# Down projection of six token tiles from seven block products instead of eight, with loads held back in the order pass

## The chip, the cores and the metric

The kernel runs on one core of one Trainium2 chip. The metric is the device time of one execution in microseconds (us), the median over runs. A core has five engines that run side by side, each with its own instruction list that it works through in order: TensorE (PE: matmuls, and PEld, its weight loads), VectorE (DVE), ScalarE (ACT), GpSimd (POOL) and SyncE (SP). In this kernel SP issues every DMA. Data lie in device memory, in the on-chip buffer SBUF (128 partitions), and matmuls write to PSUM, which has 8 banks of 128 partitions x 512 floats.

## The reference, cut to what matters

One inference step of a two-part layer (a token mixer, then a gated feed-forward block with a causal convolution) on 1024 prompt tokens and 32 sample tokens, all in float32. The change lies in the last matrix product.

```
def conv_ffn(xn, buf, w_up, conv_w, conv_b, w_down):
    up = xn @ w_up                                  # 1024 -> 2 * 2816
    up, buf = causal_dwconv(up, buf, conv_w, conv_b)
    gate, val = jnp.split(up, 2, axis=-1)
    return (jax.nn.gelu(gate, approximate=True) * val) @ w_down, buf   # 2816 -> 1024
...
x = x + rms_norm(h, g_mix_post[l])
h, ffn_buf = conv_ffn(rms_norm(x, g_ffn_pre[l]), states[6][l], ffn_w_up[l], ffn_conv_w[l], ffn_conv_b[l], ffn_w_down[l])
x = x + rms_norm(h, g_ffn_post[l])
```

## The kernel before, in words

**Tiles.** The 1056 tokens are nine tiles `u`: 0 to 7 are 128 prompt tokens each, 8 is the 32 sample tokens. The 2816 hidden features are `NF` = 22 tiles `f` of 128. Every float32 matrix product is done as three matmuls of rounded halves (`mm3`, L87 to L89): an operand is split into a high half (a cast on ACT, L93) and the remainder (a subtraction on DVE, L96). So each operand of a product costs one ACT and one DVE instruction before PE can use it.

**Stages.** By time: input projection and token mixer with the output projection (0 to about 640 us), up projection (about 640 to 1104 us), down projection (from 1096 us to the end).

**Up projection** (`up_block`, `up_finish`). For each `f` the gate tile and the value tile are computed in a seven-product form over two column ranges (`SUBS`) into `uu`; it is kept in `puy`, `pux`, `puw`, `puz` of PSUM and added out by DVE (L1197). `up_finish` then copies halo columns (POOL, L1229 to L1232), does the three-tap convolution (ACT L1233, two DVE L1235 per half), the GELU (ACT L1237), the product (DVE L1238), and stores the result of 128 features x 1060 columns to device memory as `h_d[f]` (L1239). `up_operands` makes the operand sums for the next `f` (DVE L1163 to L1169) and their splits.

**Down projection** (`down_all`). Three token groups (`DGROUPS`) are worked through one after the other, each over all 22 `f`. For every `f`, `load_h` loads the group's columns of `h_d[f]` into `hr` and the 128 x 1024 weight tile into `wd_..r` (L1302, L1307), both with two buffers, and splits them: one split of `hr`, two of the weight tile.

- The first group (tiles 0, 1 and the 32 sample tokens, 288 columns) has the weights as the stationary operand: 8 banks `pd` of 128 output features x 288 columns, 24 matmuls per `f`. Its result is copied to `accd`, turned by PE transposes (`pt`, L1350) and finished.
- The second and third group (tiles 2 to 4, tiles 5 to 7) have the tokens as the stationary operand: 6 banks `pd` of 128 tokens x 512 output features, 18 matmuls per `f`, 22 times.

`finish` (L1289 to L1297) squares a tile's result on ACT, multiplies by the gain `gp` on DVE, forms the reciprocal root on POOL (L207, L208), scales and adds the residual `fr` on DVE, and stores it.

**What sets the order.** The program is first recorded in the order of the Python code. Then `order` builds a graph of the instructions and `play` walks it as a list scheduler with fixed costs: each engine takes, among the instructions that are ready, the one with the longest remaining path (`tails`; `AHEAD` adds to the priority of some pools). The resulting sequence is fixed for every engine, SP's list of DMAs among them. An engine never reorders at run time: when the next instruction waits, everything behind it on that engine waits too. In `play`, `queue` stands for the time at which all DMAs issued so far would be through.

Of the kernel before, what the change touches and what calls it, by code (L numbers as in the profile page):

```python
# [36 lines left out]
DGROUPS = [(0, 1, 8), (2, 3, 4), (5, 6, 7)]  # L37
# [40 lines left out]
def body(ctx: ExitStack, tc: tile.TileContext, a: dict):  # L78
# [47 lines left out]
    h_d = dr.tile([NF, 128, NCOL], F32, name="h_d")  # L126

# [1094 lines left out]

    def up_finish(py, f, uu):

        ys = []
        for i, j in enumerate((f, NF + f)):
            u = uu[i][:, 2:]
            y = py.tile([128, NCOL], F32, tag="y", name=f"y{j}", bufs=3)
# [10 lines left out]
        sp.dma_start(h_d[f], ys[0])  # L1239

# [31 lines left out]
    def down_all(ph, p6, gp):  # L1272
        xres = {}

        def residual(u):
            n = 128 if u < 8 else DEC
            x = p6.tile([128, 1024], F32, tag="xres", name=f"fr{u}", bufs=4)
            sp.dma_start(x[:n], x2_d[128 * u:128 * u + n, :])
            xres[u] = x

        def finish(u, n, src):

            x = xres.pop(u)
            ss = p6.tile([128, 4], F32, tag="fss", name=f"gss{u}", bufs=2)
            jk = p6.tile([128, 1024], BF16, tag="fjk", name=f"gjk{u}", bufs=2)
            ys = []
            for hf in range(2):
                c = slice(512 * hf, 512 * hf + 512)
                act.activation(jk[:n, c], src[hf], AF.Square, scale=1.0 / 32, accum_out=ss[:n, 2 + hf:3 + hf])  # L1289
                y = p6.tile([128, 512], F32, tag="yt", name=f"yt{u}{hf}", bufs=4)  # L1290
                dve.tensor_tensor(y[:n], src[hf], gp[:n, c], op=ALU.mult)
                ys.append(y)
# [6 lines left out]
        def load_h(g, f, spans, w):  # L1299
            r = ph.tile([128, 384], F32, tag="hr", name=f"hr{g}_{f}", bufs=2)  # L1300
            for (c0, c1, o) in spans:
                sp.dma_start(r[:, o:o + c1 - c0], h_d[f, :, c0:c1])  # L1302
            hh = ph.tile([128, 384], F32R, tag="hh", name=f"hh{g}_{f}", bufs=2)
            hl = ph.tile([128, 384], F32R, tag="hl", name=f"hl{g}_{f}", bufs=2)
            split(hh[:, :w], hl[:, :w], r[:, :w], dve)
            wr = praw[0].tile([128, 1024], F32, tag="raw", name=f"wd{g}_{f}r", bufs=2)
            sp.dma_start(wr, a["w_dn"][f])  # L1307
            return hh, hl, [weight_halves(f"wd{g}_{f}{hf}", wr[:, 512 * hf:512 * hf + 512]) for hf in range(2)]

        def spans_of(us):  # L1310
            spans, off, w = [], {}, 0
            for u in us:
                n = 128 if u < 8 else DEC
                off[u] = w
                if spans and spans[-1][1] == fcol(u):
                    spans[-1][1] += n
                else:
                    spans.append([fcol(u), fcol(u) + n, w])
                w += n
            return spans, off, w  # L1320

        def banks_of(g, m):

            where = [(psf, "xw", 4)] * 4 + [(psb, "big", 3)] * 3 + [(psf, "sx", 1)]
            return [p.tile([128, 512], F32, tag=t, name=f"pd{g}_{i}", bufs=b) for i, (p, t, b) in enumerate(where[:m])]


        us = DGROUPS[0]
        spans, off, w = spans_of(us)
        banks = banks_of(0, 8)  # L1330
        for f in range(NF):
            hh, hl, wd = load_h(0, f, spans, w)
            if f == NF - 4:
                for u in us:
# [4 lines left out]
        acc = p6.tile([128, 8, 288], F32, name="accd")  # L1339
        for d in range(8):  # L1340
            (act.copy if d % 2 else dve.tensor_copy)(acc[:, d, :], banks[d][:, :w])

        def turned(u):
            n = 128 if u < 8 else DEC
            src = []
            for hf in range(2):
                p, t, b = ((psb, "big", 3), (psf, "sx", 1))[hf]
                ps = p.tile([128, 512], F32, tag=t, name=f"pt{u}{hf}", bufs=b)
                for d in range(4):
                    pe.transpose(ps[:n, 128 * d:128 * d + 128], acc[:, 4 * hf + d, off[u]:off[u] + n], ident)  # L1350
# [670 lines left out]
```

## Time and profile before

| | |
|---|---|
| median of 3 runs | 1376.55 us (1372.03, 1376.55, 1376.82) |
| the profiled execution | 1371.32 us |
| its span, first to last instruction | 1369.5 us |
| mean granted TensorE clock | 0.997 of full |
| PE busy, share of span | 1324.6 us, 97% |
| DVE busy, share of span | 986.7 us, 72% |
| ACT busy, share of span | 702.2 us, 51% |
| DMA | 255.13 MB, mean 186 GB/s |

The profile is of one execution, which took 1371.32 us; its span is 1.8 us shorter. A row of the groups reads: line, engine, operation, output tile <- input tiles, shapes, count | busy us, mean ns of one | idle time of the engine before them and what ended it. Successive instructions of one engine overlap, so the mean ns of one is longer than the distance from start to start. A row of the stretches gives for each piece of the span the busy time of PE, PEld, DVE, ACT and POOL with the number of instructions in brackets, then the granted clock, the busy share of the DMA engines and the rate in GB/s.

### The profile page before, as it was taken

How to read it: one execution, taken by the hardware profiler on the slowest of the kernel's cores; microseconds unless marked ns; L12 is line 12 of the kernel's file. 1: busy time of each engine (PE TensorE's matmuls, PEld its weight loads, DVE VectorE, ACT ScalarE, POOL GpSimd, SP SyncE). 2: the span in 40 equal slices, each digit the busy share in tenths (PEclk: the TensorE clock that was granted, in tenths of full speed). 3: DMA queues.
4: the chain of work that ended last, by engine and by line, in shares of the span. 5: the costliest groups of instructions: out<-in, count | busy, mean ns of one | idle time of the engine just before them, and what ended most of it. 6: DMA issues, size and time to landing. Idle time of an engine off the chain costs nothing.

```text
span 1369.5 us, 30222 instructions
## 1 busy us (share of the span) xinstructions
PE 1324.6 (97%) x12076; PEld 1223.9 (89%) x12076; DVE 986.7 (72%) x1765; ACT 702.2 (51%) x1369; POOL 171.8 (13%) x331
## 2 busy tenths in 40 slices
PE   6999999999999899999899999999999999999998
PEld 5999999998899777778899999999999999888786
DVE  6785549757888477877988887887887765545644
ACT  5554566445575454436654454454454455444443
POOL 2010001100102012222011111111111100000200
PEclk9999999999999999999999999999999999999999
DMA  8899789986898863634122221222221377656853
GB/s 319 270 330 323 249 279 316 295 262 196 312 298 274 299 225 116 211 107 157 48 91 82 80 79 71 86 78 71 87 78 67 106 239 228 193 170 190 291 176 102
DMA packets 130851, 255.13 MB, mean 186 GB/s; under 512 B 28087, under 2 KB 76887, under 8 KB 130711
## 3 DMA queue, kind: packets, MB, share of 16 engines
q1 hardware_dynamic: 130711, 253.21, 55.5%
q8 instruction: 94, 1.54, 0.5%
q14 instruction: 46, 0.38, 0.1%
HBM read 192.01 MB, written 61.16 MB: 185 GB/s over the span
## 4 chain that ended last, share of the span: by engine, by line
PE 80%; DVE 8%; DMA 7%; ACT 2%; issue 1%; SPq 0%; POOL 0%; DVEq 0%; ACTq 0%; POOLq 0%
PE pd L87 6%; PE pd L88 6%; PE pd L89 6%; PE pux L89 4%; PE pux L87 4%; PE pux L88 4%; PE pv L87 4%; PE pv L89 4%; PE pv L88 4%; PE puw L88 3%; PE puw L89 3%; PE puw L87 3%; PE pf L87 3%; PE pf L89 3%; PE pf L88 3%; PE zp L87 2%
## 5 line engine op out<-in xcount | busy, mean ns | idle before, releaser
L1235 DVE SCALAR_TENSOR_TENSOR y<-uu,fconv_sb,y 128x1060 f32<-128x1060 f32 x88 | 116.1, 1321 | 11.2 <-ACT y L1233 10.5
L87 PE MATMUL pd<-wd,hh 128*128 128x512 f32 x264 | 77.8, 396 | 0.7 <-ACT hh L93 0.7
L88 PE MATMUL pd<-wd,hh 128*128 128x512 f32 x264 | 77.8, 396 | 0.0
L89 PE MATMUL pd<-wd,hl 128*128 128x512 f32 x264 | 77.0, 396 | 0.0
L1233 ACT ACTIVATE y<-uu,fconv_sb 128x1060 f32<-128x1060 f32 x44 | 56.0, 1275 | 20.1 <-POOL uu L1230 20.1
L922 POOL TENSOR_TENSOR hrs<-hss,mhalf 128x5 f32<-128x5 f32 (+3 forms) x27 | 40.5, 1505 | 180.9 <-DVE hss L921 180.9
L96 DVE TENSOR_TENSOR hl<-hr,hh 128x384 fp32r<-128x384 f32 (+1 forms) x66 | 34.5, 523 | 39.1 <-PE pd L89 23.7
L87 PEld LDWEIGHTS pd<-wd,hh 128*128 128x128 f32 x264 | 49.4, 188 | 13.2 <-ACT hh L93 1.1
L89 PEld LDWEIGHTS pd<-wd,hl 128*128 128x128 f32 x264 | 49.3, 188 | 12.0
L88 PEld LDWEIGHTS pd<-wd,hh 128*128 128x128 f32 x264 | 49.4, 188 | 11.7
L1192 ACT COPY c<-pux 128x274 f32<-128x274 f32 (+1 forms) x132 | 46.0, 381 | 25.1 <-PE pux L89 24.3
L87 PE MATMUL pv<-wt_0h,xh 128*128 128x256 f32 (+2 forms) x195 | 53.3, 298 | 3.4 <-DVE xl L305 1.7
L93 ACT CAST hh<-hr 128x384 fp32r<-128x384 f32 (+1 forms) x66 | 32.0, 486 | 43.1 <-PE pd L88 30.2
L89 PE MATMUL pv<-wt_0h,xl 128*128 128x256 f32 (+2 forms) x195 | 51.3, 289 | 0.0
L88 PE MATMUL pv<-wt_0l,xh 128*128 128x256 f32 (+2 forms) x195 | 51.2, 287 | 0.0
L87 PE MATMUL pv<-wt_1h,xh 128*128 128x256 f32 (+2 forms) x195 | 49.1, 288 | 0.4 <-ACT xh L304 0.4
L89 PE MATMUL pv<-wt_1h,xl 128*128 128x256 f32 (+2 forms) x195 | 48.6, 289 | 0.8 <-DVE xl L305 0.8
L88 PE MATMUL pv<-wt_1l,xh 128*128 128x256 f32 (+2 forms) x195 | 48.1, 287 | 0.0
L1230 POOL COPY uu<-fcache_sb 128x2 f32<-128x2 f32 x44 | 16.1, 366 | 192.0 <-DVE uu L1197 192.0
L87 PEld LDWEIGHTS pv<-wt_0h,xh 128*128 128x128 f32 (+1 forms) x195 | 34.9, 189 | 5.4 <-DVE xl L305 1.8
L207 POOL TENSOR_SCALAR gss<-gss 128x1 f32<-128x1 f32 (+1 forms) x9 | 6.7, 745 | 243.8 <-ACT gjk L1289 243.8
L89 PEld LDWEIGHTS pv<-wt_0h,xl 128*128 128x128 f32 (+1 forms) x195 | 34.9, 189 | 0.7 <-DVE xl L305 0.2
(1720 smaller groups left out, 4971.4 us busy)
## 6 DMA issues: line engine op xcount, KB each, us to landing
h_d<-y SPq DMA_DIRECT2D x22, 530.0 KB, 2.8
wt_0r<-in_w_tok SPq DMA_DIRECT2D x21, 512.0 KB, 6.1
wt_1r<-in_w_tok SPq DMA_DIRECT2D x21, 512.0 KB, 5.7
wt_0l<-lt_d SPq DMA_DIRECT2D x14, 512.0 KB, 7.5
wt_1l<-lt_d SPq DMA_DIRECT2D x14, 512.0 KB, 5.9
qkb<-qkb_d SPq DMA_DIRECT2D x8, 768.0 KB, 7.5
hr<-h_d SPq DMA_DIRECT2D x44, 128.0 KB, 3.1
hr<-h_d SPq DMA_DIRECT2D x22, 192.0 KB, 3.4
```

Of the source, the lines that this page charges most:

```text
L87: pe.matmul(ps, lh[0], rh[0], start=first, stop=False, **kw)
L88: pe.matmul(ps, lh[0], rh[1], start=False, stop=False, **kw)
L89: return pe.matmul(ps, lh[1], rh[0], start=False, stop=last, **kw)
L93: act.copy(hi, src)
L96: (eng or pool).tensor_tensor(lo, src, hi.bitcast(F32), op=ALU.subtract)
L207: pool.tensor_scalar(out, ss, other, EPS, op0=ALU.add, op1=ALU.add)
L922: pool.tensor_tensor(rs[:n, h0:h0 + nh], ss[:n, h0:h0 + nh], mhalf[:n, :nh], op=ALU.pow)
L1192: act.copy(t, ps)
L1230: pool.tensor_copy(u[:, GAP_S:GAP_S + 2], fcache[:, j, :])
L1233: act.activation(y, u, AF.Identity, scale=fconv[:, j, 2:3], bias=fconv[:, j, 3:4])
L1235: dve.scalar_tensor_tensor(y, uu[i][:, s:s + NCOL], fconv[:, j, s:s + 1], y, op0=ALU.mult, op1=ALU.add)
```

## The change

Tokens are regrouped: the first group is now tiles 0, 8 and 4 (`FIRST`), still done in the direct form. Tiles 1 to 3 (`UPPER`) and 5 to 7 (`LOWER`) are done together as a 2 x 2 block product: rows are upper and lower tokens, the inner dimension is taken in `NP` = 11 pairs of `f` (even and odd), and the columns are the two halves of the 1024 outputs. The eight block products of the direct form are replaced by seven products of sums of blocks (`seven`, called for p1, p2, p6, p5, p3, p7, p4), each over 11 pairs and three token tiles.

- **Sums of the left operand** are made in `up_finish` after every odd `f`: four DVE instructions on 128 x 384, stored as `s_d`.
- **Sums of the weights** are made by `sums`: four DVE instructions on 128 x 512 and two stores of 512 KB to `t_d` per pair. Six pairs are done during the up projection from two extra loads each (`EARLY`), five during the first group from the weight tiles that are loaded there anyway.
- **Loads of the passes**: 128 x 384 of the left operand and 128 x 512 of the right into one tile `r` with three buffers; one split of each.
- **Results** are combined from PSUM by ACT copies and DVE additions into `cu` and `cl`, and finished in halves (`finish_half`, `finish_end`).
- **Buffers**: the weight tiles of the first group rotate over 4 new `wide` buffers (the first two over the old pair), pools change sides, `gp` and the residuals of the first group are requested two `f` earlier, the product tile `y` of the value half has one buffer of its own.
- **The order pass**: names get priorities of their own (`AHEAD`), and SP takes no further DMA while the modelled DMA backlog is more than `BACKLOG` = 2000 ns. This holds for the whole program, so lists of the earlier stages change as well.

```diff
-DGROUPS = [(0, 1, 8), (2, 3, 4), (5, 6, 7)]
+FIRST, UPPER, LOWER = (0, 8, 4), (1, 2, 3), (5, 6, 7)
+NP = NF // 2
+EARLY = (0, 2, 4, 5, 7, 9)
...
+    def sums(k, ws):
+        (b11, b12), (b21, b22) = ((t[:, :512], t[:, 512:]) for t in ws)
+        dve.tensor_tensor(b11, b12, b11, op=ALU.subtract)
+        dve.tensor_tensor(b12, b22, b12, op=ALU.subtract)
+        dve.tensor_tensor(b22, b22, b11, op=ALU.subtract)
+        dve.tensor_tensor(b21, b21, b22, op=ALU.subtract)
+        for i in range(2):
+            sp.dma_start(t_d[k, i], ws[i])
...
         sp.dma_start(h_d[f], ys[0])
+        if f % 2 == 0:
+            even[0] = ys[0]
+            return
+        (a11, a21), (a12, a22) = ([t[:, fcol(us[0]):fcol(us[0]) + 384] for us in (UPPER, LOWER)] for t in (even[0], ys[0]))
+        st = py.tile([128, 3, 384], F32, tag="st", name=f"st{f}", bufs=1)
+        s1, s2, s3, s4 = st[:, 0], a11, st[:, 1], st[:, 2]
+        dve.tensor_tensor(s1, a21, a22, op=ALU.add)
+        dve.tensor_tensor(s3, a11, a21, op=ALU.subtract)
+        dve.tensor_tensor(s2, s1, a11, op=ALU.subtract)
+        dve.tensor_tensor(s4, a12, s2, op=ALU.subtract)
+        sp.dma_start(s_d[f // 2, :, 0:3], st)
+        sp.dma_start(s_d[f // 2, :, 3], s2)
+        if (f // 2) in EARLY:
+            k = EARLY.index(f // 2)
+            ws = [py.tile([128, 1024], F32, tag="bw", name=f"bw{2 * k + i}", bufs=2) for i in range(2)]
+            for i in range(2):
+                sp.dma_start(ws[i], a["w_dn"][2 * k + i])
+            sums(k, ws)
...
+            wr = praw[0].tile([128, 1024], F32, tag="raw", name=f"wd0_{f}r", bufs=2) if f < 2 else                 wide(f"wd0_{f}r")
             sp.dma_start(wr, a["w_dn"][f])
...
+            pair.append(wr)
+            if f % 2:
+                if f // 2 >= len(EARLY):
+                    sums(f // 2, pair)
+                pair = []
...
-        for g, us2 in enumerate(DGROUPS[1:], 1):
...
-                    for hf in range(2):
-                        mm3(banks[2 * i + hf], (hh[:, c], hl[:, c]), wd[hf], f == 0, f == NF - 1)
...
+        def seven(p, ps, first):
+            ops = []
+            for k in range(NP):
+                r = ph.tile([128, NCOL], F32, tag="y0", name=f"r{p}_{k}", bufs=3)
+                sp.dma_start(r[:, :384], ASRC[p](k))
+                sp.dma_start(r[:, 384:896], BSRC[p](k))
+                hh, hl = h_halves(f"{p}_{k}", 384, r[:, :384], *((ph, "h") if k % 2 else (p6, "g")))
+                wd = weight_halves(f"wd{p}_{k}", r[:, 384:896])
+                ops.append((k, hh, hl, wd))
+                if k == NP - 2:
+                    continue
+                for i in range(3):
+                    c = slice(128 * i, 128 * i + 128)
+                    for (j, hh, hl, wd) in ops:
+                        mm3(ps[i], (hh[:, c], hl[:, c]), wd, first and j == 0, j == NP - 1, skip_group_check=True)
+                ops = []
+                if k % 3 == 0 and todo:
+                    todo.pop(0)()
...
+        seven("p1", x, True)
...
+        for i in range(3):
+            act.copy(c11[i], x[i])
+        y = three("y")
+        seven("p2", y, True)
+        for i in range(3):
+            dve.tensor_tensor(c11[i], c11[i], y[i], op=ALU.add)
+        seven("p6", x, False)
...
+        seven("p5", w_, True)
+        for i in range(3):
+            act.copy(c22[i], w_[i])
+        seven("p3", w_, False)
+        for i, u in enumerate(UPPER):
+            dve.tensor_tensor(c12[i], c12[i], w_[i], op=ALU.add)
+            finish(u, 128, (c11[i], c12[i]))
+        seven("p7", x, False)
...
+        for i, u in enumerate(LOWER):
+            dve.tensor_tensor(c22[i], c22[i], x[i], op=ALU.add)
+            finish_half(u, 128, 1, c22[i])
+        seven("p4", x, False)
+        for i, u in enumerate(LOWER):
+            finish_half(u, 128, 0, x[i])
+            finish_end(u, 128)
...
+BACKLOG = 2000.
-AHEAD = {"mx": 10000., "psm": 10000.}
+AHEAD = {"mx": 10000., "psm": 10000., "pdx0": 1400., "pdx1": 700., "pdw0": 1400., "pdw1": 700., "pt": 130000.}
...
+        if e == "SP" and queue - t - 1400 > BACKLOG:
+            heapq.heappush(ready[e], c)
+            free[e] = queue - 1400 - BACKLOG + 5
+            continue
```

The tables below show rows of the fixed lists, as the order pass leaves them, at three places. A row is line, operation, output tile <- inputs, shape; the line numbers of the second list are those of the changed file.

**SP, output projection of the mixer.** `wor` are the output weights (512 KB each), `wt_7_1` is the last weight tile of the input projection, `lt_d` holds low halves, `v_d` and `g_d` take results of that projection, `ct` are mixer results for the output projection. Before:

```order
L318 DMA wt_6_1l<-lt_d 128x1024
L401 DMA v_d<-vg_3_6498 128x256
L401 DMA v_d<-vg_3_6530 128x256
L651 DMA wor_6207<-in_w_out 128x1024
L401 DMA v_d<-vg_3_6536 32x256
L651 DMA wor_6209<-in_w_out 128x1024
L651 DMA wor_6211<-in_w_out 128x1024
L651 DMA wor_6213<-in_w_out 128x1024
L651 DMA wor_6215<-in_w_out 128x1024
L651 DMA wor_6217<-in_w_out 128x1024
L256 DMA ct_6219<-cat_d 128x1024
```

Now:

```order
L322 DMA wt_6_1l<-lt_d 128x1024
L405 DMA v_d<-vg_3_6500 128x256
L405 DMA v_d<-vg_3_6532 128x256
L405 DMA v_d<-vg_3_6538 32x256
L655 DMA wor_6209<-in_w_out 128x1024
L655 DMA wor_6211<-in_w_out 128x1024
L655 DMA wor_6213<-in_w_out 128x1024
L655 DMA wor_6215<-in_w_out 128x1024
L322 DMA wt_7_0l<-lt_d 128x1024
L415 DMA g_d<-vg_4_6583 128x256
L322 DMA wt_7_1l<-lt_d 128x1024
L655 DMA wor_6217<-in_w_out 128x1024
```

Six weight loads stood in a row ahead of the operands `wt_7`; now four do, and two come behind them.

**DVE, up projection, tile f = 2**, from the last operand sum to the splits of the next tile's operands (`S_3h`). Before:

```order
L1169 TENSOR_TENSOR wu3r<-wu3r 128x512
L96 TENSOR_TENSOR hl_1_14390<-hr_1_14386,hh_1_14389 128x288
L1197 TENSOR_TENSOR uu_8824<-c_20_9473,puw_0_9433 128x274
L1197 TENSOR_TENSOR uu_8825<-c_20_9538,puz_0_9448 128x274
L96 TENSOR_TENSOR S_3h<-wu25r,S_3h 128x512
```

Now:

```order
L1263 TENSOR_TENSOR y_9152<-st_9419,y_9152 128x384
L1173 TENSOR_TENSOR wu3r<-wu3r 128x512
L1264 TENSOR_TENSOR st_9419<-y_9400,y_9152 128x384
L1201 TENSOR_TENSOR uu_8826<-c_20_9492,puw_0_9452 128x274
L1232 TENSOR_TENSOR bw_10442<-bw_10443,bw_10442 128x512
L1201 TENSOR_TENSOR uu_8827<-c_20_9557,puz_0_9467 128x274
L98 TENSOR_TENSOR S_3h<-wu25r,S_3h 128x512
```

Sums of the left operand (L1263, L1264) and of the weights (L1232) now stand among the additions that free PSUM and ahead of the splits.

**SP, first group of the down projection, f from 12 on.** Before:

```order
L1307 DMA wd_16r<-in_w_dn 128x1024
L1302 DMA hr_15_14932<-h_d 128x256
L1302 DMA hr_15_14932<-h_d 128x32
L1307 DMA wd_17r<-in_w_dn 128x1024
L1302 DMA hr_16_14971<-h_d 128x256
```

Now:

```order
L1236 DMA t_d<-wd_14r 128x1024
L1360 DMA hr_15136<-h_d 128x128 x2
L1236 DMA t_d<-wd_15r 128x1024
L1360 DMA hr_15136<-h_d 128x32
L1363 DMA wd_18r<-in_w_dn 128x1024
L1236 DMA t_d<-wd_16r 128x1024
L1360 DMA hr_15183<-h_d 128x128 x2
L1360 DMA hr_15183<-h_d 128x32
L1363 DMA wd_19r<-in_w_dn 128x1024
```

The stores of the sums now stand in SP's list among the loads; the load of `wd_18r` takes the buffer that the store of `wd_14r` just above it has to leave.

More of the change, by code (lines that the diff above doesn't have):

```diff
@@ L126, in body @@
     h_d = dr.tile([NF, 128, NCOL], F32, name="h_d")
+    s_d = dr.tile([NP, 128, 4, 384], F32, name="s_d")
+    t_d = dr.tile([NP, 2, 128, 1024], F32, name="t_d")
     lf_d = dr.tile([13, 128, 8, 128], F32R, name="lf_d")
@@ L1310, in spans_of @@
[L1310 to L1325, printed above, removed]
@@ L1328, in down_all, with finish, h_halves @@
[L1328 to L1334, printed above, removed]
+        def finish(u, n, src):
+            for hf in range(2):
+                finish_half(u, n, hf, src[hf])
+            finish_end(u, n)
+        def h_halves(name, w, r, pool_, tag):
+            hh, hl = (pool_.tile([128, 384], F32R, tag=f"{tag}{x}", name=f"h{x}{name}", bufs=2) for x in "hl")
+            split(hh[:, :w], hl[:, :w], r, dve)
+            return hh, hl
@@ new lines, in down_all @@
+        off, w = {}, 0
+        for u in FIRST:
+            off[u] = w
+            w += 128 if u < 8 else DEC
+        where = [(psf, "xw", 4)] * 4 + [(psb, "big", 3)] * 3 + [(psf, "sx", 1)]
+        banks = [p.tile([128, 512], F32, tag=t, name=f"pd0_{i}", bufs=b) for i, (p, t, b) in enumerate(where)]
+        pair = []
+        for f in range(NF):
+            r = ph.tile([128, 288], F32, tag="hr", name=f"hr{f}", bufs=2)
+            for u in FIRST:
+                n = 128 if u < 8 else DEC
+                sp.dma_start(r[:, off[u]:off[u] + n], h_d[f, :, fcol(u):fcol(u) + n])
+            hh, hl = h_halves(f"0_{f}", w, r, ph, "h")
+            wr = praw[0].tile([128, 1024], F32, tag="raw", name=f"wd0_{f}r", bufs=2) if f < 2 else                 wide(f"wd0_{f}r")
+            sp.dma_start(wr, a["w_dn"][f])
+            wd = [weight_halves(f"wd0_{f}{hf}", wr[:, 512 * hf:512 * hf + 512]) for hf in range(2)]
+            pair.append(wr)
+            if f % 2:
+                if f // 2 >= len(EARLY):
+                    sums(f // 2, pair)
+                pair = []
+            if f == NF - 6:
+                sp.dma_start(gp, a["grows"][1:2, :].broadcast_to([128, 1024]))
+                for u in FIRST:
@@ L1338, in down_all @@
                 mm3(banks[d][:, :w], [t[:, c] for t in wd[d // 4]], (hh[:, :w], hl[:, :w]), f == 0, f == NF - 1)
-        acc = p6.tile([128, 8, 288], F32, name="accd")
+        accs = p6.tile([128, 8, 288], F32, name="accd")
+        accs = [accs[:, d] for d in range(8)]
         for d in range(8):
-            (act.copy if d % 2 else dve.tensor_copy)(acc[:, d, :], banks[d][:, :w])
+            (act.copy if d % 2 else dve.tensor_copy)(accs[d], banks[d][:, :w])
+        x = [psf.tile([128, 512], F32, tag="xw", name=f"pdx{i}", bufs=4) for i in range(3)]
@@ new lines, in three @@
+        def three(name):
+            return [psb.tile([128, 512], F32, tag="big", name=f"pd{name}{i}", bufs=3) for i in range(3)]
+        seven("p1", x, True)
+        cu = [wide(f"cu{u}") for u in UPPER]
+        cl = [praw[0].tile([128, 1024], F32, tag="raw", name=f"cl{i}", bufs=2) for i in range(2)]
+        c11, c12 = ([t[:, 512 * hf:512 * hf + 512] for t in cu] for hf in range(2))
+        c22 = [cl[0][:, :512], cl[0][:, 512:], cl[1][:, :512]]
+        for i in range(3):
+            act.copy(c11[i], x[i])
@@ new lines, in down_all @@
+        y = three("y")
[4 more added lines that the diff above has]
+        for i in range(3):
+            act.copy(c12[i], x[i])
+        for u in UPPER:
+            residual(u)
+        w_ = three("w")
+        seven("p5", w_, True)
+        for i in range(3):
+            act.copy(c22[i], w_[i])
[3 more added lines that the diff above has]
+            finish(u, 128, (c11[i], c12[i]))
```

88 lines of the change are left out of this document (41 added, 47 removed).

## The prediction

> **What bounds the kernel now.** I read the busy times and the chain of waits first, then the busy time by stretches, then single groups and pieces of the timeline at the places that the change touches. The page:
>
> ```profile
> PE 1324.6 (97%) x12076; PEld 1223.9 (89%) x12076; DVE 986.7 (72%) x1765; ACT 702.2 (51%) x1369; POOL 171.8 (13%) x331
> PE 80%; DVE 8%; DMA 7%; ACT 2%; issue 1%; SPq 0%; POOL 0%; DVEq 0%; ACTq 0%; POOLq 0%
> ```
>
> PE is busy for all but 44.9 of 1369.5 us and holds 80% of the chain that ends last. An average can hide stages with other limits, so the stretches:
>
> ```profile
> 20.00:40.00 20.00, 18.23 (x119) 15.71 (x119) 14.11 (x21) 12.47 (x24) 3.60 (x8) 1.00 0.97 358
> 100.00:120.00 20.00, 19.78 (x167) 19.55 (x166) 13.55 (x24) 10.64 (x25) 0.00 (x0) 1.00 0.99 346
> ...
> 440.00:460.00 20.00, 15.68 (x126) 14.64 (x125) 6.17 (x25) 8.23 (x26) 1.16 (x1) 0.91 0.83 274
> 460.00:480.00 20.00, 17.79 (x139) 16.37 (x138) 10.39 (x29) 9.56 (x24) 2.74 (x2) 0.91 0.74 272
> ...
> 640.00:660.00 20.00, 15.12 (x111) 13.62 (x110) 12.49 (x15) 15.97 (x34) 3.06 (x7) 1.00 0.35 112
> ```
>
> ```profile
> 670.00:800.00 130.00, 129.98 (x1060) 129.76 (x1059) 109.84 (x159) 68.44 (x119) 20.36 (x56) 1.00 0.25 87
> 800.00:950.00 150.00, 150.00 (x1226) 150.00 (x1225) 121.60 (x177) 74.15 (x132) 21.67 (x57) 1.00 0.22 79
> ...
> 1095.00:1115.00 20.00, 18.75 (x144) 18.34 (x142) 14.24 (x21) 9.40 (x18) 2.31 (x8) 1.00 0.68 234
> 1115.00:1173.00 58.00, 56.65 (x425) 56.60 (x425) 34.44 (x59) 30.58 (x59) 0.00 (x0) 1.00 0.74 228
> ...
> 1180.00:1250.00 70.00, 70.00 (x302) 56.31 (x301) 31.79 (x50) 29.42 (x51) 0.00 (x0) 1.00 0.55 172
> 1250.00:1290.00 40.00, 39.32 (x181) 31.08 (x180) 30.02 (x49) 20.59 (x48) 11.17 (x12) 1.00 0.82 275
> ```
>
> From 670 us on PE has no gap to speak of. In the up projection DVE is the next engine (84% busy, 109.84 of 130), in the first group of the down projection DMA (0.74), in the two other groups nothing comes near PE. So a matmul that goes away there shortens the run, as long as DVE and DMA can carry what is added.
>
> **The change part by part.** *The products removed.* The two groups of 512 columns are
>
> ```profile
> L87 PE MATMUL pd<-wd,hh 128*128 128x512 f32 x264 | 77.8, 396 | 0.7 <-ACT hh L93 0.7
> 1333.39 1.40 PE pd L87 x6
> 1334.79 1.40 PE pd L88 x6
> ```
>
> three lines of 264, 792 matmuls, 1.40 / 6 = 233.3 ns from start to start (the 396 ns of one overlap). That is 184.8 us. Now 7 passes x 11 pairs x 3 tiles x 3 = 693 of the same shape: 161.7 us. **-23.1 us**. The Trainium skill (TensorE: Matmul & The Clock Gate, Back-to-back issue gap) gives columns / 2.4 + 2.5 ns, 215.8 ns at 512; by it the 99 matmuls were worth 21.4 us, but the trace's 233.3 ns decides. The first group keeps its 528 matmuls of 288 columns (56.65 us for 425, 133.3 ns each, 3.2 us per `f`), and the 24 transposes stay.
>
> *The passes.* A step is 9 matmuls, 2.10 us of PE, and now needs its own loads of 256 and 192 KB through three buffers `r`. What such a round costs shows where the old loads were catching up, with two buffers:
>
> ```profile
> 1293.78 0.33 SPq L1307 DMA_DIRECT2D wd_9r<-in_w_dn  x1
> 1297.37 1.14 ACT L93 CAST wd<-wd_9r 128x512 fp32r<-128x512 f32 x2 [1.20 <-DMA wd_9r<-in_w_dn]
> 1298.03 1.29 DVE L96 TENSOR_TENSOR wd<-wd_9r,wd 128x512 fp32r<-128x512 f32 x2 [0.99 <-ACT wd L93]
> 1299.35 0.33 SPq L1307 DMA_DIRECT2D wd_11r<-in_w_dn  x1
> ```
>
> Issue to issue into the same buffer takes 5.57 us: 3.59 from issue to the cast, the rest casts and subtractions. `r` also holds the tokens, whose split comes behind:
>
> ```profile
> L96 DVE TENSOR_TENSOR hl<-hr,hh 128x384 fp32r<-128x384 f32 x44 | 24.5, 557 | 32.6 <-PE pd L89 23.7 <-ACT hh L93 3.6 <-issue 3.3
> ```
>
> 5.57 + 0.56 = 6.13 us, over three buffers 2.04 us per step, just under 2.10; the loads are smaller (448 KB against 704), which leaves a little more. The rate is 459 kB / 2.10 us = 218 GB/s, below the 275 that the stretch from 1250 us carried. DVE per pass: 11 x (0.69 + 0.56) = 13.7 of 23.1 us; in p1 and p7, where finished tiles come in, about 10 us more, still under 23.1. SP has two issues of 0.33 us per step. So the passes keep PE's pace, hidden behind its 2.10 us, with a margin of 0.06 us a step by the bound and more by size. Bounds 0 and +52 (below, first rival); I take **+1.0**, near the row of catching up, since steady loads are what it shows.
>
> *The first group.* Added are 20 DVE sums (5 pairs x 4), ten stores of 512 KB, and `hr` in three pieces. Work of DVE: 34.4 of 58 us plus 12 leaves room. DMA is closer. For f = 12 to 21, 32 us of PE: ten `hr` 1.5 MB, six weight tiles 3.1, ten stores 5.2, three `r` 1.4, in all 11.2 MB or 351 GB/s. The rows at 20 and 100 us show 358 and 346 at a share of 0.97 to 0.99, the row of the same kind of loads 228 / 0.74 = 308. A `wide` buffer's round: 5.57 for load and split, 1.3 for the partner's split, 4 x 0.60 of sums, and the store,
>
> ```profile
> h_d<-y SPq DMA_DIRECT2D x22, 530.0 KB, 2.8
> ```
>
> 12.1 us against 4 x 3.2 = 12.8. Both sit at the limit. SP issues in order: a late sum holds back its store `t_d`, and behind it stand the `hr` loads that PE waits for. Bounds: -2.6 (four more buffers could remove the 1.25 and 1.35 us that PE idles in 1095 to 1173) and +7 (11.2 MB at 308 GB/s is 4.5 us over, and one round of a late buffer); I take **+2.5**.
>
> *The up projection.* PE needs 168 matmuls per `f`, 150.00 / 1226 x 168 = 20.55 us; DVE has 28.4 / 7.3 = 3.9 us free per `f`. Added: 2 sums of 384 per `f` on average, and 24 sums of 512 for `EARLY`. One takes
>
> ```profile
> 701.62 0.68 DVE L1163 TENSOR_TENSOR wu25r<-wu25r 128x512 f32<-128x512 f32 x1
> 702.22 0.41 DVE L1197 TENSOR_TENSOR uu<-c,puy 128x256 f32<-128x256 f32 x1
> ```
>
> 0.60 us start to start, one of 384 some 0.48. Spread out that would be 1.6 us per `f`. But the new DVE list has all 24 within the first six tiles: 24 x 0.60 + 12 x 0.48 = 20.1 us against 20.2 us that DVE is idle in 670 to 800, 6.3 tiles. There DVE is full; from the seventh tile on 1.0 of 3.9 us is used. Cover is that PE reads the operands one tile later than they are made (`S_3h` in tile 2); gone, every us of DVE shows on PE. Bounds 0 and +20.1; **+2.0**, near the low end, for the gaps are idle by rows and the sums only fill them.
>
> *The order pass.* Early lists change without a matmul more or less. The stall at 440 to 480 us (PE idle 4.3 + 2.2, granted clock 0.91) stands in the chain as
>
> ```profile
> 450.66 7.39 DMA wt_1r<-in_w_tok
> 458.07 7.86 DMA wor<-in_w_out
> 465.99 6.82 DMA g_d<-vg
> ```
>
> a queue of loads. Two of the six `wor` now come behind `wt_7_1l`: 1.05 MB at 274 GB/s, 3.8 us earlier. Elsewhere orders swap with no row that prices them. Bounds: -13 (the idle 1.8 at 20, 6.5 at 440, 4.9 at 640 all gone) and +6.5 (the stall once more); I take **-2.5**.
>
> *The end.* After the last matmul
>
> ```profile
> 1362.40 0.40 PE L89 MATMUL pd<-wd,hl 128*128 128x512 f32 x1
> ...
> 1364.60 2.07 DVE L1296 SCALAR_TENSOR_TENSOR fr<-yt,gss,fr 128x512 f32<-128x512 f32 x3
> ```
>
> three results queue on DVE; now half of each tile is prepared before. At most one instruction less: **-0.5** (bounds -0.7 and 0).
>
> Sum: -23.1 + 1.0 + 2.5 + 2.0 - 2.5 - 0.5 = **-20.6 us**. Against the profiled execution (1371.3, span 1369.5) that is 1350.7. The four known executions are 1371.3, 1372.0, 1376.6 and 1376.8; their middle is 1374.3, and I forecast a median of **1354**.
>
> **The rivals.** *The passes wait for their loads (slower).* In the stretch where results are written, a load of the same 192 KB took longer:
>
> ```profile
> hr<-h_d SPq DMA_DIRECT2D x7, 192.0 KB, 5.8
> ```
>
> Then the round is 6.13 - 3.59 + 5.8 = 8.34 us, 2.78 per step, 77 steps 214 us: 52 us over the 161.7, 29 over the old 184.8. With the other terms (+1.5) that is 1374.3 + 30.5 = 1405. It decides from a landing of 3.8 us on (6.30 us round), and eats the whole gain at 4.7. For it: the margin is thin. Against: 5.8 belongs to a share of 0.82 with residuals and results in the queue; the steady stretch 1180 to 1250 carried 704 KB per 4.2 us without a gap. The Trainium skill (DMA: Bandwidth & Descriptors, Bandwidth) speaks for this rival: it advises at least 1 MiB per DMA, and lists 64 KB in 0.95 us and 1 MB in 6.15; in between, as an estimate, 256 and 192 KB one after the other take 3.6 us, above 2.10. By that rule, an estimate again, 704 KB would take about 5 us, yet they came every 2.8, so loads overlap.
>
> *Crowded DMA at two places.* The first group loses the full 7, and p1 and p7 (22 steps) run at 2.78: +15. Sum -23.1 + 7 + 15 + 2.0 - 2.5 - 0.5 = -2.1: 1372.
>
> *DVE becomes the bound of the early up projection.* If its gaps are waits that cannot be filled, the 20.1 us land on PE: -23.1 + 1.0 + 2.5 + 20.1 - 2.5 - 0.5 = -2.5: 1372. For it: the free time and the work added are equal. Against: later tiles have 3.9 us to catch up, and PE stood still for 0.02 of the 280 us of the two rows above.
>
> *The order pass does not do what it says.* Loads held back arrive late in the early stages, +6.5 instead of -2.5: 1363.
>
> **How the numbers follow.** Forecast 0.66, order pass 0.12, crowded DMA 0.10, DVE 0.08, passes behind their loads 0.04. A measurement of this kernel tells about 0.5% (6.9 us) from no change. Forecast and order pass are faster, and the two cases at 1372 scatter to both sides of 1369.7, four parts in ten below: 0.78 + 0.07 = 0.85 faster; slower are the last case and the rare tails, 0.05; the same 0.10. The forecast's own range is 1347 to 1361 (its terms at -27 and -13). For 8 in 10 it has to take in the order pass at 1363 and some of the crowded cases, and below, half of the early gain left open: **1345 to 1367**.
>
> **What would show it.** Right: in the new profile 693 matmuls of 128x512 at 233 ns; passes of 23.1 us with PE busy throughout; PE idle under 5 us in the first group; DVE at 95% or more in the first six tiles of the up projection with PE still without gaps; less idle PE around 450 us. Wrong: ACT casts that wait for DMA `r` in the passes and a step above 2.2 us (first rival); PE waiting for `hh` with SP standing at a `t_d` store; PE waiting for DVE splits or freed banks between 670 and 800 us; new PE idle before 640 us. If the passes are clean and the time is still above 1367, the place is one that I have not priced.

## The result and the profile after

The changed kernel takes 1356.7 us (median; 1356.2 to 1357.8) against 1374.3 us before on the same chip: a ratio of 0.988, 95% interval 0.984 to 0.992, or 17.6 us less. The forecast was 1354 in a range of 1345 to 1367. The profiled execution took 1356.24 us with a span of 1354.4, 15.1 us less than the span before.

The page of the changed kernel, busy times and the chain of waits by engine:

```profile
PE 1303.9 (96%) x11977; PEld 1207.9 (89%) x11977; DVE 1039.2 (77%) x1884; ACT 710.6 (52%) x1400; POOL 181.9 (13%) x331
PE 69%; DMA 14%; DVE 9%; ACT 4%; issue 3%; SPq 1%; POOL 0%; DVEq 0%; ACTq 0%; POOLq 0%
```

PE is busy 20.7 us less. But DMA has gone from 7% to 14% of the chain and PE from 80% to 69%: there is a place where loads now set the end. Groups and DMA issues of the same page say which (last number of an issue: median us from issue to landing):

```profile
L95 ACT CAST wdp<-rp 128x512 fp32r<-128x512 f32 x77 | 47.7, 620 | 70.4 <-DMA rp<-t_d 39.0
...
rp<-t_d SPq DMA_DIRECT2D x44, 256.0 KB, 3.8
...
rp<-in_w_dn SPq DMA_DIRECT2D x33, 256.0 KB, 3.7
rp<-s_d SPq DMA_DIRECT2D x44, 192.0 KB, 3.9
```

The casts of the passes stand waiting for loads 39 us for one source alone. By the page the loads land after 3.7 to 3.9 us, where the forecast had taken 3.59 from the catching-up row and put the turning point at 3.8. But the page's medians rest on few loads, 6 of the 44 from `t_d` and 5 of the 33 from `w_dn`; by the semaphore updates that the trace holds for all 77 weight loads the median is 3.6 us and the mean 3.9. A single load lands about as forecast. A step has two, though, issued mostly 0.4 us apart, and from the first issue until both are there 4.4 us pass (mean of the 69 steps whose loads are issued from 1171 us on).

The waits of PE between 1171 and 1347 us, the seven passes (total, times, longest):

```profile
PE pdx L89 <- ACT hhp L95: 4.6, 4, 2.0
PE pdx L89 <- DVE cl L1454: 2.1, 1, 2.1
PE pdw L89 <- ACT hhp L95: 1.7, 1, 1.7
PE pdw L89 <- ACT cl L1445: 0.8, 1, 0.8
PE pdy L89 <- ACT hhp L95: 0.2, 1, 0.2
```

9.4 us in eight pieces, the long ones where one pass hands over to the next. The stretches of the up projection, of the first group and of two passes:

```profile
670.00:800.00 130.00, 129.66 (x1056) 129.41 (x1056) 123.85 (x191) 66.86 (x117) 30.71 (x53) 1.00 0.56 196
800.00:950.00 150.00, 150.00 (x1225) 150.00 (x1224) 129.08 (x191) 73.31 (x131) 22.18 (x57) 1.00 0.27 97
...
1115.00:1173.00 58.00, 55.74 (x410) 54.13 (x409) 45.33 (x79) 27.19 (x54) 0.00 (x0) 1.00 0.89 291
...
1222.00:1246.00 24.00, 21.53 (x93) 17.15 (x94) 15.12 (x26) 12.20 (x24) 0.00 (x0) 1.00 0.62 199
```

DVE carries its sums (123.85 of 130 us) and PE has 0.34 us of gaps there; the first group idles 2.26 us. In the passes the DMA engines are only 62% busy while PE waits: the rate is not the limit, but the time that the loads of one step take.

**How one late load holds up two steps.** SP, ACT and PE where pass p6 hands over to p5 (start, length; in brackets the idle time before and what ended it):

```profile
1244.22 0.32 SPq L1409 DMA_DIRECT2D rp<-t_d  x1
...
1245.76 0.37 SPq L1409 DMA_DIRECT2D rp<-t_d  x1
...
1252.18 0.32 SPq L1409 DMA_DIRECT2D rp<-t_d  x1
```

```profile
1247.20 0.62 ACT L95 CAST wdp<-rp 128x512 fp32r<-128x512 f32 x1 [2.15 <-DMA rp<-t_d]
1247.73 0.58 ACT L1439 COPY cu<-pdx 128x512 f32<-128x512 f32 x1
1250.04 0.62 ACT L95 CAST wdp<-rp 128x512 fp32r<-128x512 f32 x1 [1.73 <-DMA rp<-t_d]
1250.57 0.58 ACT L1439 COPY cu<-pdx 128x512 f32<-128x512 f32 x1
1251.05 0.93 ACT L95 CAST hhp<-rp 128x384 fp32r<-128x384 f32 x2
```

```profile
1251.61 0.74 PE L89 MATMUL pdw<-wdp,hhp 128*128 128x512 f32 x2 [1.71 <-ACT hhp L95]
```

The weights issued at 1244.22 were there at 1247.20, the tokens of the same step at 1248.94 (the last semaphore update of their load). But the cast of these tokens stands in ACT's list behind the weight cast of the next step, whose load (1245.76) landed only at 1250.04. So PE waits for a cast whose input had been there for 2.1 us, and the buffer is free, and its next load issued, at 1252.18: a round of 7.96 us. Over the 69 steps the mean round is 6.9 us: 4.4 until both loads are there, 2.4 from then to the last subtraction, 0.1 to the next issue. The passes take 175.0 us (first to last matmul), 2.27 a step, where 693 matmuls alone are 157.1.

**A second stall, and half the clock behind it.** DVE and PE where p7 hands its banks to p4:

```profile
1320.28 0.69 DVE L98 TENSOR_TENSOR wdp<-rp,wdp 128x512 fp32r<-128x512 f32 x1 [2.18 <-ACT wdp L95]
1320.89 0.55 DVE L98 TENSOR_TENSOR hlp<-rp,hhp 128x384 fp32r<-128x384 f32 x1
1321.36 0.68 DVE L1454 TENSOR_TENSOR cl<-cl,pdx 128x512 f32<-128x512 f32 x1
...
1322.18 0.47 PE L89 MATMUL pdx<-wdp,hhp 128*128 128x512 f32 x1 [2.12 <-DVE cl L1454]
...
1323.62 0.63 PE L90 MATMUL pdx<-wdp,hhp 128*128 128x512 f32 x1
...
1324.05 0.63 PE L89 MATMUL pdx<-wdp,hhp 128*128 128x512 f32 x1
...
1324.48 0.63 PE L90 MATMUL pdx<-wdp,hhp 128*128 128x512 f32 x1
```

```profile
1321.00:1327.00 6.00, 4.82 (x14) 3.85 (x15) 5.93 (x11) 4.41 (x11) 0.00 (x0) 0.72 1.03 383
```

The addition that frees the bank (L1454) stands behind a split whose load is late; DVE itself idles 2.18 us. From 1 us behind the 2.12 us gap the granted clock is 0.5 for 3.4 us (0.72 in the stretch), and matmuls start every 0.43 us instead of 0.227: eight of them, 1.6 us in all. The Trainium skill (TensorE: Matmul & The Clock Gate, HAM oscillation) asks for no idle gaps above about 3.4 us; here a shorter one was followed by the half rate. It need not be: in the second profile of the changed kernel (below) the same wait is longer and the pace stays,

```profile
1320.43 0.47 PE L89 MATMUL pdx<-wdp,hhp 128*128 128x512 f32 x1 [2.17 <-DVE cl L1454]
...
1322.12 0.40 PE L90 MATMUL pdx<-wdp,hhp 128*128 128x512 f32 x1
1322.35 0.62 PE L91 MATMUL pdx<-wdp,hlp 128*128 128x512 f32 x2
```

with 0.23 us from start to start. Behind 660 us all profiles of this study together hold 26 gaps of PE of 1.4 to 2.7 us; 8 were followed by half the clock and 18 were not. What decides it, these runs do not show.

### The profile page after: what moved, and what is told of

The parts are those of the page before. It is cut to its first block, busy times and chain, and to the rows that moved or that the text cites. A ratio compares the mean times of both kernels' runs of the same rounds, so it can differ in the third digit from the quotient of the medians.

```text
span 1354.4 us, 30370 instructions
## 1 busy us (share of the span) xinstructions
PE 1303.9 (96%) x11977; PEld 1207.9 (89%) x11977; DVE 1039.2 (77%) x1884; ACT 710.6 (52%) x1400; POOL 181.9 (13%) x331
## 4 chain that ended last, share of the span: by engine, by line
PE 69%; DMA 14%; DVE 9%; ACT 4%; issue 3%; SPq 1%; POOL 0%; DVEq 0%; ACTq 0%; POOLq 0%
PE pux L91 4%; PE pux L89 4%; PE pux L90 4%; PE pv L89 4%; PE pv L91 4%; PE pv L90 4%; DMA rp<-t_d 4%; PE pf L89 3%; PE pf L91 3%; PE pf L90 3%; PE puw L90 3%; PE puw L91 3%; PE puw L89 3%; DMA rp<-in_w_dn 2%; PE zp L89 2%
## 5 line engine op out<-in xcount | busy, mean ns | idle before, releaser
L98 DVE TENSOR_TENSOR wdp<-rp,wdp 128x512 fp32r<-128x512 f32 x77 | 53.2, 691 | 56.2 <-ACT wdp L95 55.9
L95 ACT CAST wdp<-rp 128x512 fp32r<-128x512 f32 x77 | 47.7, 620 | 70.4 <-DMA rp<-t_d 39.0
L926 POOL TENSOR_TENSOR hrs<-hss,mhalf 128x5 f32<-128x5 f32 (+3 forms) x27 | 35.8, 1330 | 175.3 <-DVE hss L925 172.6
L89 PE MATMUL pdx<-wdp,hhp 128*128 128x512 f32 x132 | 44.8, 404 | 6.7 <-ACT hhp L95 4.6
L1245 POOL COPY uu<-fcache_sb 128x2 f32<-128x2 f32 x44 | 23.4, 531 | 186.1 <-DVE uu L1201 186.1
L98 DVE TENSOR_TENSOR hlp<-rp,hhp 128x384 fp32r<-128x384 f32 x77 | 41.8, 552 | 5.4 <-ACT hhp L95 2.9
L90 PE MATMUL pdx<-wdp,hhp 128*128 128x512 f32 x132 | 43.9, 395 | 0.0
L91 PE MATMUL pdx<-wdp,hlp 128*128 128x512 f32 x132 | 42.9, 395 | 0.1
L95 ACT CAST hhp<-rp 128x384 fp32r<-128x384 f32 x77 | 38.4, 511 | 5.8 <-PE pdx L90 3.1
L89 PEld LDWEIGHTS pdx<-wdp,hhp 128*128 128x128 f32 x132 | 24.8, 191 | 13.9 <-ACT hhp L95 6.7
L808 DVE COPY_PREDICATED P<-masks_sb,sc 128x352 f32<-128x352 int32 (+1 forms) x44 | 29.8, 678 | 8.8 <-PE sc L773 8.3
```

What stands on the lines that cost most here:

```text
L89: pe.matmul(ps, lh[0], rh[0], start=first, stop=False, **kw)
L90: pe.matmul(ps, lh[0], rh[1], start=False, stop=False, **kw)
L91: return pe.matmul(ps, lh[1], rh[0], start=False, stop=last, **kw)
L95: act.copy(hi, src)
L98: (eng or pool).tensor_tensor(lo, src, hi.bitcast(F32), op=ALU.subtract)
L808: dve.copy_predicated(dst, mk_.broadcast_to([n, 11, *mk_.shape[2:]]), src)
```

## The experiments

Every kernel here computes the whole result. Ratios are to the kernel before on the same chip; with them the absolute medians.

**The changed kernel again** (no edit), as the base for the next three.

> The changed kernel again, beside the variants on one chip. Ratio to the kernel before 0.988 (1356.7 / 1374.3); between 0.984 and 0.992.

Measured: 1353.9 us, ratio 0.988 (0.985 to 0.991). PE idles for 2.6 us between 440 and 480 us, the passes take 172.9 us. It repeats.

**Five buffers for the loads of the passes.** The two extra ones use the space `bw` of the up projection.

```diff
-                r = ph.tile([128, NCOL], F32, tag="y0", name=f"r{p}_{k}", bufs=3)
+                tag, wd_, nb = (("y0", NCOL, 3), ("bw", 1024, 2), ("y0", NCOL, 3), ("bw", 1024, 2), ("y0", NCOL, 3))[turns[0] % 5]
+                turns[0] += 1
+                r = ph.tile([128, wd_], F32, tag=tag, name=f"r{p}_{k}", bufs=nb)
```

> The passes' loads get five buffers instead of three (two of them in the space of the weight tiles of the sums, which is free by then). PE idles 9.4 us in the passes of the changed kernel. Theory A, the load round: each load is issued when one of three buffers is freed, about 6.1 to 6.8 us a round with landings of 3.6 to 4.3 us, 2.04 to 2.27 us a step against 2.10 of PE; late loads also hold up what stands behind them in ACT's and DVE's lists at the ends of the passes. With five buffers 1.2 to 1.4 us a step, so nearly all 9.4 us and 1.6 us of lowered clock go: 9 to 11 us less than the changed kernel, and no waits of ACT's casts for DMA in the passes to speak of. Theory B, the handing over between passes (copies, squares and additions in ACT's and DVE's lists): only the 4.7 us that end on a late load go, the 0.8 + 1.8 + 2.1 us at handing over stay: 4 to 5 us less. Theory C, the DMA engines are the limit and more requests in flight only land later: 0 to 2 us less.

Measured: 1342.1 us, ratio 0.980 (0.977 to 0.982), 11.7 us less than the changed kernel beside it. Theory A's 9 to 11, slightly passed. Of the page: the chain, the casts, two issues; then all waits of PE in the passes:

```profile
PE 81%; DVE 7%; DMA 6%; ACT 3%; issue 2%; POOL 1%; SPq 0%; DVEq 0%; ACTq 0%; POOLq 0%
...
L95 ACT CAST wdp<-rp 128x512 fp32r<-128x512 f32 x77 | 47.3, 621 | 38.2 <-DMA rp<-t_d 19.5
...
rp<-t_d SPq DMA_DIRECT2D x44, 256.0 KB, 5.3
...
rp<-in_w_dn SPq DMA_DIRECT2D x33, 256.0 KB, 4.4
```

```profile
PE pdx L89 <- DVE cl L1458: 0.7, 1, 0.7
PE pdx L89 <- ACT hhp L95: 0.3, 1, 0.3
```

PE waits 1.0 us instead of 9.4, and the passes take 162.0 us, 10.9 less than in the run beside it. The waits at handing over went with the others, so theory B falls: those lists were only late because a load was. PE's busy time falls as well, from 1303.9 and 1303.7 us in the two profiles of the changed kernel to 1300.8, for as many matmuls. The half clock is 1.6 us of that in the first profile and nothing in the second, whose passes ran at the full granted clock; the rest is late starts that do not show as idle time, since a matmul counts as busy for 0.39 us and the next can start after 0.227. Theory C falls too: the run got 11.7 us shorter, and the loads do not even land later. By the semaphore updates of all 77 weight loads the median is 3.6 us, as with three buffers; the 5.3 and 4.4 of the page are medians of four and five loads. One part of A was wrong: casts still wait for loads at times, only ahead of need. The order pass plans the lists anew for five buffers, so buffers and order change together in this run.

**Two buffers.**

```diff
-                r = ph.tile([128, NCOL], F32, tag="y0", name=f"r{p}_{k}", bufs=3)
+                r = ph.tile([128, 1024], F32, tag="bw", name=f"r{p}_{k}", bufs=2)
```

> The passes' loads get two buffers instead of three. Theory A: a round of 6.1 to 6.8 us over two buffers, 3.05 to 3.4 us a step, 77 steps: 73 to 100 us more than the changed kernel. Theory B: the loads have slack and only the handing over costs: under 10 us more. Theory C, the rate is the limit: landings get shorter with fewer loads in flight, under 3 us, a round of 5.4, 2.7 a step: up to 46 us more.

Measured, in one run: 1384.5 us, 30.6 more than the changed kernel; passes of 201.6 us, a mean round of 5.4 us, 2.7 a step. The direction is A's, the size is not:

```profile
rp<-t_d SPq DMA_DIRECT2D x44, 256.0 KB, 2.9
...
rp<-in_w_dn SPq DMA_DIRECT2D x33, 256.0 KB, 3.1
```

With two buffers each load lands sooner: by all 77 weight loads the median is 3.1 us, against 3.6 with three and with five. Both loads of a step are there after 3.9 us instead of 4.4, and 1.5 instead of 2.4 us pass from then to the last subtraction: the weight cast of the next step stands between a step's two casts less often (0.6 instead of 1.5 us from the one to the other). Theory A had kept the round of three. C's figure for the step (2.7 us) came right, though as the bound of a rate it is refuted by the five buffers.

**No hold-back**, and below it **the hold-back alone** on the kernel before.

```diff
-BACKLOG = 2000.
+BACKLOG = 1e9
```

> The changed kernel with the hold-back of loads in the order pass taken out (BACKLOG beyond reach), for all stages. If the hold-back is what removed the stall of 440 to 480 us and brought the up projection forward by 3.2 us: that stage is back at 3 to 4 us later, and the run 3 us longer in that part. If the lists of the early stages changed for other reasons, the up projection begins where it does now and the run differs by under 1 us. In the passes loads are issued as soon as a buffer is free in either case, so no difference there is expected beyond 2 us.

Measured: 1351.9 us, ratio 0.988 (0.985 to 0.992) against 0.988 with it: no difference.

```diff
+        if e == "SP" and queue - t - 1400 > 2000.:
+            heapq.heappush(ready[e], c)
+            free[e] = queue - 1400 - 2000. + 5
+            continue
         if e == "Pool" and lock and port["DVE"] > t:
```

> The kernel before with the hold-back of loads in the order pass alone (2000 ns), no products or stages changed. By the forecast's term the stall at 440 to 480 us shrinks and the up projection begins some 3 us earlier: 2 to 4 us less than before. By the run without the hold-back, which was as fast as with it (a difference of 2 us inside both intervals), there is no effect: within 2 us of before, with the start of the up projection where the scatter of single profiles (632 to 636 us for equal early lists) has it.

> The kernel before once more, for a second profile: its time within 0.5% of before, and a second reading of the start of the up projection (637.1 us in the first) and of the idle time of PE from 440 to 480 us (6.5 us). If these repeat within 1 us, the 3.2 us between the two profiles are the order's; if they scatter by 3 us, a single profile cannot tell.

Measured: alone 1369.7 us, ratio 0.998 (0.996 to 1.000), 2.7 us less with an interval from 5.4 to nothing; the kernel before again 1371.4 us, with its start 1.9 us earlier than in its first profile, between the two limits named. Two kernels below that have the same early lists start at 631.2 and 632.5 us, so a single profile cannot tell. **Five buffers without the hold-back**:

> The changed kernel with five buffers and without the hold-back of loads in the order pass. With three buffers the hold-back made no difference that could be told (0.9882 without, 0.9881 with), alone on the kernel before it was worth 2.7 us (interval 0 to 5.4). If it is worth that in any lists: 2 to 3 us more than five buffers alone (0.9795), with the up projection beginning later. If it is worth nothing: within 2 us; the start of the up projection inside the 632 to 636 us where single profiles scatter.

Measured: 1343.4 us, ratio 0.980 (0.978 to 0.982) against 0.980 with it. So it is worth nothing that can be told in the changed kernel. Its page also gives shorter landings for five buffers, on 12 and 10 loads, than the page of the other five-buffer run on four and five:

```profile
rp<-t_d SPq DMA_DIRECT2D x44, 256.0 KB, 3.4
...
rp<-in_w_dn SPq DMA_DIRECT2D x33, 256.0 KB, 3.5
```

The starts of the up projection (the number ahead of "to") of the kernel before again, of the hold-back alone, and of five buffers without it:

```profile
L87 PE MATMUL pux<-B11h,A_0h x8: 283/288/354, 635.1 to 651.4; 128*128 128x274 f32 x4, 128*128 128x256 f32 x4
```

```profile
L87 PE MATMUL pux<-B11h,A_0h x8: 281/288/353, 633.8 to 650.3; 128*128 128x274 f32 x4, 128*128 128x256 f32 x4
```

```profile
L89 PE MATMUL pux<-B11h,A_0h x8: 283/288/355, 635.5 to 652.0; 128*128 128x274 f32 x4, 128*128 128x256 f32 x4
```

Over all profiles of this study the start lies at 631.2 to 637.1 us in six profiles without the hold-back (mean 633.8) and at 632.1 to 637.3 in eight with it (mean 634.3). The idle time of PE at 440 to 480 us does shrink, from a mean of 5.0 us without (2.9 to 6.5) to 3.1 with (1.9 to 4.3). Since the start does not move with it, what is saved there is lost again before 630 us; where, was not looked into.

**All weight sums in the up projection, and all in the first group**, both with five buffers.

```diff
-EARLY = (0, 2, 4, 5, 7, 9)
+EARLY = tuple(range(11))
```

> With the five buffers of the earlier run, and the weight sums of all eleven pairs in the up projection instead of six (none in the first group). Up projection: 20 sums of 0.60 us more on DVE, 12 us, where DVE idles 5 of 130, 21 of 150 and 25 of 145 us after 670 us. If its gaps can be filled (the forecast's +2.0 is mostly cover), PE has no new gaps and the stage ends where it did. If they are waits that cannot be filled, up to 12 us show on PE. First group: ten stores of 512 KB and 12 us of DVE less; if those hold back the loads there, the 2.7 us that PE idles from 1095 to 1173 us shrink to about 1, so 1 to 2 us less than with five buffers alone; if not, no difference.

Measured: 1341.8 us, ratio 0.977 (0.974 to 0.980); the interval overlaps that of five buffers alone, so no difference that can be told. The first group idles 1.3 instead of 2.7 us from 1115 to 1173, as expected, and PE gets 0.8 us of new gaps from 800 to 950 us: DVE's gaps can be filled almost for free.

```diff
-EARLY = (0, 2, 4, 5, 7, 9)
+EARLY = ()
```

> With the five buffers, and the weight sums of all eleven pairs in the first group (none in the up projection). First group: twelve more stores of 512 KB (6.3 MB) and 24 sums (14.4 us of DVE) in 80 us that already move 299 GB/s, 23.9 MB. If DMA bounds that stage (the forecast's term of 2.5, the rival of crowded DMA), 30.2 MB at the 326 to 351 GB/s seen at most take 86 to 93 us: 6 to 13 us more, with PE waiting for the split of the tokens behind late loads. If the stage has room, under 2 us more. Up projection: 14.4 us of DVE and 12 MB less, PE has no gaps there already, so under 0.5 us less.

Measured: 1358.4 us, ratio 0.990 (0.987 to 0.993), 1.05% or 14 us more than five buffers alone (9.5 between the two profiles). The first group, and in it PE's waits:

```profile
1095.00:1115.00 20.00, 18.00 (x126) 17.76 (x125) 17.80 (x31) 10.33 (x18) 7.56 (x5) 0.91 0.96 321
1115.00:1173.00 58.00, 50.61 (x350) 49.05 (x349) 47.53 (x80) 23.49 (x45) 0.00 (x0) 0.94 0.97 326
```

```profile
PE pd L89 <- ACT hh L95: 6.6, 4, 2.7
PE pd L90 <- DVE hl L98: 2.6, 2, 2.0
```

DMA is nearly full (0.97 at 326 GB/s), PE waits 9.2 us for the tokens' split, and the granted clock falls to half three times for 3.4 us (0.91 and 0.94 in the rows). So the stage has no room for eleven pairs. That DMA is what bounds it fits the rows, but is not shown by itself: SP also stands up to 3.3 us for a sum of DVE ahead of its store. With five pairs PE idles 2.26 us there.

**The pace of the matmuls.** With five buffers the matmuls of 128x512 start every 226.7 ns; in the kernel before every 233.3, in all of its profiles, at the same granted clock. Shapes are equal, and in pass p2 the order is too. What differs is where the split halves of the tokens, the stationary operand, begin in SBUF: 224 bytes beyond a multiple of 512 before, 320 now, which is also where the halves of the weights, the moving operand, begin in both kernels. Three kernels move them; the lists of the engines stay word for word. The first moves nothing else. In the other two, neighbours of the halves move along (in the third `y` and `hr`, in the second also `st`, `bw`, the loads `rp` and small tiles of `finish`), but PE reads none of these in its matmuls of 128x512.

```diff
-            hh = ph.tile([128, 384], F32R, tag="hh", name=f"hh{g}_{f}", bufs=2)
+            hh = ph.tile([128, 400], F32R, tag="hh", name=f"hh{g}_{f}", bufs=2)[:, 8:392]
```

(and `hl` alike; in the changed kernel the same in `h_halves`)

> The kernel before, with nothing moved but the split halves of the tokens in the down projection: their tiles get 32 bytes ahead of the data, so each begins on a multiple of 64 bytes in SBUF instead of 32 beyond one. The lists of all engines are the same. In its two groups of 512 columns the tokens are the stationary operand, and matmuls start every 233.3 ns there in all three profiles of this kernel; in the changed kernel and its variants they start every 226.7 ns, with the same shapes, in the same order in pass p2, but with the halves on multiples of 64 bytes. Theory of the address: 226.7 ns here too, 792 x 6.67 ns = 5.3 us less than before. Theory that something else in the changed kernel sets the pace (banks, neighbours on the other engines): 233.3 ns, no difference.

Measured: ratio 0.997 (0.996 to 0.999); the pace is 230.6 to 232 ns in most of the two groups. Less than the theory gave: it had named multiples of 64 as the condition, and with that met the pace came only some 40% of the way.

> The changed kernel with five buffers, and the halves of the tokens moved 32 bytes off a multiple of 64 bytes, in the first group and in the passes; all lists the same. Theory of the address: the 693 matmuls of the passes start every 233.3 ns, 4.6 us more than with five buffers alone; without a stall to hide in it shows in full. Other theory: 226.7 ns and no difference.

Measured: 1344.6 us, ratio 0.981 (0.979 to 0.984), an interval that overlaps that of five buffers alone, so the 4.6 us do not show in the time; but the pace is 231.6 to 233.2 ns. The address matters in this direction too, nearly in full.

```diff
-            y = py.tile([128, NCOL], F32, tag="y", name=f"y{j}", bufs=3)
+            y = py.tile([128, NCOL + 8], F32, tag="y", name=f"y{j}", bufs=3)[:, :NCOL]
```

> The kernel before, again with nothing moved but the split halves of the tokens: a buffer ahead of them is 96 bytes longer in all, so that all four of their tiles begin 320 bytes beyond a multiple of 512, which is where the halves of the weights (the moving operand) begin and where both begin in the changed kernel. In the kernel before they began at 224; in the run that shifted them by 32 bytes at 256, 352, 448 and 32 plus 32, so mixed, and the pace was 230.6 to 231 ns. If the address explains the whole of the pace: 226.7 ns in the two groups of 512 columns, 792 x 6.67 ns = 5.3 us less than before. If only a part of it: 229 to 231 ns, 2 to 3 us less. If something else does: 233.3 ns.

(The earlier shift had put the tiles at 256, 320, 384 and 448, not as listed there.) Measured: 1365.2 us, ratio 0.996 (0.994 to 0.997), 6 us less than before. Before, and in phase, three matmuls per row:

```profile
1200.02 0.86 PE L88 MATMUL pd<-wd,hh 128*128 128x512 f32 x3
1200.72 0.86 PE L89 MATMUL pd<-wd,hl 128*128 128x512 f32 x3
```

```profile
1198.25 0.84 PE L87 MATMUL pd<-wd,hh 128*128 128x512 f32 x3
1198.93 0.84 PE L88 MATMUL pd<-wd,hh 128*128 128x512 f32 x3
```

0.70 us against 0.68 for three, 226.7 ns: the address explains all of it. Whether it has to agree with the moving operand's, or with a fixed grid, these runs don't tell.

## Why the prediction was right, and where it was not

The time fell inside the range and on the forecast side. The terms, by the two spans (-15.1 us, forecast -20.6):

- *The products removed*, forecast -23.1: mis-sized by the pace. 792 at 233.3 ns were 184.8 us, but the 693 run at 226.7: 157.1, so **-27.7**. 4.6 us of the change's gain come from where a tile happens to lie; the kernel before gets 6 us from the same shift of 96 bytes. The Trainium skill's 215.8 ns (TensorE: Matmul & The Clock Gate, Back-to-back issue gap), which the page gives for a single isolated matmul, fits neither pace.
- *The passes*, forecast +1.0: **about +13.1** (the rest of the 14.6 us by which the stretch from the last matmul of the first group to the last of all got shorter). 9.4 us are waits of PE, 1.6 the half clock behind one of them, most of the rest late starts that do not count as idle. This is the term that was mis-sized. The mechanism was named, the round over three buffers, but it was priced at 6.13 us from a row with one load: 3.59 from issue to cast and 2.54 of casts and subtractions. Here the two loads of a step are both there only after 4.4 us; with 2.4 us behind them and 0.1 to the next issue the round is 6.9, above the 6.3 that three steps of PE were to take. So the margin of 0.06 us a step was none. The 2.4 are no more than forecast, but the two-buffer run needs 1.5, so about 0.9 of them come from the casts of two steps standing interleaved in ACT's list. The first rival had the right place: casts waited for loads and "a step above 2.2 us", named as the sign of being wrong, came with 2.27. Its 2.78 us a step did not come, and a single landing lies only at its turning point of 3.8 us (mean 3.9, median 3.6), not at its 5.8.
- *The first group* and *the up projection*, forecast +2.5 and +2.0: together **+1.7** (from the start of the up projection to the last matmul of the group 537.4 us before, 539.1 now), which cannot be told from nothing: the second profile of before has 539.5. DVE at 95% in the first six tiles with PE without gaps came as forecast; the DVE rival fell. A crowded first group, the second rival, costs time once all eleven pairs are put there, not before.
- *The order pass*, forecast -2.5: -3.2 by the two profiles, but that start scatters by 5 us and more among kernels with equal lists up to there, and two comparisons with and without show nothing. The stall shrinks at its place; that it shortens the run is not shown.
- *The end*, forecast -0.5: **+0.9**, the span ends 8.0 us after the start of the last matmul, against 7.1 before. Why it grew stays open. DVE still ends on three results in a row,

```profile
1348.89 2.07 DVE L1335 SCALAR_TENSOR_TENSOR fr<-yt,gss,fr 128x512 f32<-128x512 f32 x3
```

as before; what was prepared earlier didn't shorten that queue.

Sum: -27.7 + 13.1 + 1.7 - 3.2 + 0.9 = -15.2, beside -15.1 measured. So the good forecast is partly luck: 12.1 us of cost missed in the passes stood against 4.6 us of gain missed in the products and 2.8 us of cost too much for the first group and the up projection. The Trainium skill's single loads one after the other (DMA: Bandwidth & Descriptors, Bandwidth), an estimate of 3.6 us a step in the forecast, are not what bounds the passes: with five buffers a step takes 2.10 us.

## What to carry to other kernels

A round of loads that is worth 97% of the compute step is no cover: price the landing until the last load of a step is there, not that of one load, count what stands between the landing and the release of the buffer in each engine's list, and give one or two buffers more before counting the gain; here they were free, in space that an earlier stage had left. A median on a page can rest on few loads: look how many before building on it. Idle time of PE in the passes came in few long pieces at the handing over, but its cause was the round of the loads, for it went with more buffers: look at what is late on the engine ahead of the handing over before changing the handing over. When a change moves pools about, compare the start-to-start pace of matmuls that should be equal.

## What was not expected of the hardware

- Matmuls of 128x512 float32r start every 233.3 or 226.7 ns depending on the SBUF address of the stationary operand (a shift of 96 bytes, 792 matmuls, 6 us). The Trainium skill (TensorE: Matmul & The Clock Gate, Step-by-step: what each phase is for) says that loading the next weights takes no SBUF read bandwidth from the running matmul, by a port of its own; here the pace changes with where the stationary operand lies, by which way these runs do not tell.
- The 256 KB loads of the passes land in 3.1 us with two buffers and in 3.6 with three (medians of all 77), so fewer buffers cost less than a fixed landing gives. With five buffers it is 3.6 again.
- A PE gap of 2.12 us was followed by 3.4 us at half the granted clock, with matmuls every 0.43 instead of 0.227 us; a gap of 2.17 us at the same place of the same kernel was not.
